# A hybrid GLA and MLA decoder block on one core: how far ahead the output stage loads its gates, and which PSUM banks its second pass uses

## The chip, the cores and the metric

The kernel runs on one core of a Trainium2 chip. The metric is device time in microseconds (us); the value shown for the kernel before is the median of three runs. An execution with the profiler on is shown beside it: all rows of the trace come from that one.

## The reference

One decoder block over 2048 frames and 16 learned meta tokens, width 1024, float32. Two token mixers run side by side on the same normalised input: a gated linear attention in chunks (its projected result is y_a) and a multi-head latent attention with softmax (its heads' result, gated, is o_b below). The part that the change touches is the end:

```
y_b    = (o_b * silu(m_z)) @ mla_proj
merged = sigmoid(gate_gla) * y_a + sigmoid(gate_mla) * y_b
h      = h + merged @ w_out
out    = rms_norm(h, final_norm_g)[:, 16:]
```

## The kernel before

All matrices are float32, and every product is made of three matmuls (`mm3`): each operand is split into a rounded part `hi` (a copy by ScalarE) and the rest `lo` (a subtraction, source minus hi), and hi·hi, hi·lo and lo·hi are summed in PSUM. The last stage is the class `Output`. It has two passes.

**First pass, `merge` (L1606).** It computes mergedᵀ, the 1024 channels in 8 blocks of 128 (`mo`) and the frames in 8 tiles of 256 (`t`): 64 products of 24 matmuls, 8 contraction blocks by 3. The first two products are already done inside the last unit of the attention (`first`). The weights of `mla_proj` stay on chip. For each product three arrays of 128 x 256 move between DRAM and the chip: `gm`, the raw gate of the latent branch, `ma`, the gated linear branch (both loaded), and the merged block, which is built in the `ma` tile and stored to `d_mg`. ScalarE makes the sigmoid of `gm` in three instructions (L134 to L136: exponential, logarithm, exponential), VectorE multiplies it with the product in PSUM (L1645) and adds it to `ma` (L1646). The pools set how far loads run ahead: `gm` has three tiles, `ma` four, and the products have four accumulators of one PSUM bank each, in two pools of two (`self.pa`). A tile is reused when its last reader is done; for `ma` that is the store. The code loads `gm` and `ma` at the head of the step that needs them; a scheduler at build time then sets the final order on each engine and on the queue of SyncE (SP below), which issues every DMA here. Each engine and the queue work in that order: an entry that waits holds up all behind it.

Within the same loop `load_ob` (L1585) loads and splits the attention result for the next frame tile in four pairs of blocks, through two raw tiles (`obr`); the `lo` half of every second block is made by GpSimd, except in tile 0. `blocks` (L1672) prepares the weights of the second pass in tiles 1 to 4: it loads two rows of blocks of `w_out` (`w_up`, `w_dn`) and makes four sums `f` of them (L1681 to L1684, the last two on GpSimd), which it splits. In tiles 5 to 7 `operands` begins to load and split merged blocks for the second pass.

**Second pass, `project` (L1730).** It computes merged @ w_out by a 2 x 2 scheme with seven block products in place of eight: 8 pairs of 128 frames (`p`), 7 products each of 12 matmuls with 512 columns, named by the weight block that they read: y11, t1, t2, t3, y21, t4, y22. Their accumulators `oacc` come from a pool of four PSUM banks (`self.pb`), opened in `merge` already. VectorE adds them up into rows (`o_row`), GpSimd adds the input rows `x_in`, and norm and store follow. The weight blocks y21, t4 and y22 are loaded and split at the head of the pass; four split operands (`xp`) are made ahead of the products.

Of the kernel before, what the change touches and what calls it, by code (L numbers as in the profile page):

```python
# [10 lines left out]
F32 = mybir.dt.float32  # L11
# [28 lines left out]
def f(ap):  # L40
    return ap.bitcast(F32)
# [1496 lines left out]
class Output:  # L1538
# [8 lines left out]
    def __init__(self, tc, x, mla_proj, w_out, final_g, out, S):  # L1547
        self.tc, self.nc, self.S = tc, tc.nc, S
        self.x, self.w, self.wo, self.fg, self.out = x, mla_proj, w_out, final_g, out
        self.right, self.left, self.psum = Pools(tc, "right"), Pools(tc), Pools(tc)  # L1550
        self.psum_r = Pools(tc)
        self.xp = self.right("d_xp", 4)
        self.raws = self.right("d_raw", 2)
        self.obr = self.right("d_obr", 2)
        self.weights, self.places, self.made = None, [], 0

# [28 lines left out]
    def load_ob(self, t, k, pool):  # L1585
# [4 lines left out]
        for i in range(2):  # L1590
            raw = self.obr.tile([P, W], F32, tag="ob", name="ob_raw")
            nc.sync.dma_start(raw, self.S.tr("ob", k + i)[:, t * W:(t + 1) * W])
            hi, lo = both[:, 0, i], both[:, 1, i]
            nc.scalar.activation(hi, raw, AF.Copy)
            (nc.vector if i == 0 or t == 0 else nc.gpsimd).tensor_sub(lo, raw, f(hi))
            got.append((hi, lo))
        return got

    def main(self):
# [3 lines left out]
        self.psum.close()  # L1603
        self.psum_r.close()

    def merge(self):  # L1606
# [6 lines left out]
        pools = [self.xp, self.left("d_ob2", 4)]  # L1613
        io, mp = self.left("d_io", 3), self.left("d_mg", 4)
        self.pa.append(self.psum("d_pa2", 2, space=PSUM))
        self.pb = self.psum("d_pb", 4, space=PSUM)
        tmp = Pools(self.tc)
        self.wraw, self.sums = tmp("d_wr", 1), tmp("d_ws", 1)
        stores = []
        for t in range(NTL):  # L1620
            cols = slice(t * W, (t + 1) * W)
            ob, self.obs = self.obs, []
# [6 lines left out]
            for mo in range(KC):  # L1629
                gm = io.tile([P, W], F32, tag="gm", name="gm")  # L1630
                nc.sync.dma_start(gm, S.tr("gm", mo)[:, cols])
                sigmoid(nc, gm, gm)
                ma = mp.tile([P, W], F32, tag="ma", name="ma")
                nc.sync.dma_start(ma, S.tr("ma", mo)[:, cols])
                if t == 0:
# [3 lines left out]
                else:  # L1639
                    acc = self.pa[(mo + 1) % 2].tile([P, W], F32, tag="a", name="acc")  # L1640
                    for kc in range(KC):
                        self.product(mo, acc, ob, kc)
                while len(stores) > 1:
                    nc.sync.dma_start(*stores.pop(0))
# [27 lines left out]
    def blocks(self, kc):  # L1672
# [9 lines left out]
        nc.vector.tensor_sub(t2, y22, t1)  # L1682
        nc.gpsimd.tensor_sub(t3, t2, y11)
        nc.gpsimd.tensor_sub(t4, y21, t2)  # L1684
        self.halves("y11", kc, y11, nc.vector)
# [44 lines left out]
    def project(self):  # L1730
# [7 lines left out]
        def rows(p):  # L1738
# [6 lines left out]
            return got  # L1745

        t4 = []
        for kc in range(KH):
# [3 lines left out]
            t4.append(raw)  # L1752
        xs = {0: rows(0)}
        y22 = []
        for kc in range(KH):
            self.halves("t4", kc, t4[kc], nc.vector)
            y22.append(self.w_piece(KH + kc, 1))
        for kc in range(KH):
            self.halves("y22", kc, y22[kc], nc.vector)
        fg = cst.tile([P, D], F32, name="fg")  # L1760
        nc.sync.dma_start(fg, self.fg.partition_broadcast(P))

        later, stores = [], []

        def product(right):
            acc = self.pb.tile([P, 512], F32, tag="b", name="oacc")
            while len(self.ready) < 4:
# [145 lines left out]
```

## Time and profile before

| | |
|---|---|
| Median of 3 runs | 2603.93 us (2601.11 to 2605.45) |
| Profiled execution, its own time | 2599.82 us |
| Span of its trace | 2598.1 us |
| TensorE matmul busy in the span | 2509.2 us (97%) |
| VectorE, ScalarE, GpSimd busy | 1670.7, 1363.1, 383.6 us |
| First pass from its third product on | 2217.6 to 2421.0 us |
| Second pass, matmuls | 2421.0 to 2589.0 us |

Times inside the trace count from the start of the span. A row of the waits says which engine and line stood idle, after the arrow what ended the wait, and then total, times and the longest. A matmul's end is modelled: in a dense run the next one begins before the one before it has ended.

### The profile page before, as it was taken

What the parts mean: (1) busy time and instruction counts of PE and PEld (TensorE: products, weight loads), DVE (VectorE), ACT (ScalarE), POOL (GpSimd) and SP (SyncE); (2) the same over time, 40 slices, a digit from 0 to 9 for tenths busy, and PEclk for the clock granted to TensorE, in tenths of its full rate; (3) what the DMA queues carried; (4) which work ended last, traced back from release to release, by engine and by line L of the source; (5) the groups of instructions that cost most, each with busy time, mean ns of one, the idle gap of its engine ahead of it and who ended that gap; (6) DMA issues with size and microseconds to landing.
All of it is one profiled execution on the core that took longest, in us unless ns stands there. A gap on an engine that the chain in (4) does not pass through costs nothing. (4 is left out here: it accounts for less than half of the span.)

```text
span 2598.1 us, 42674 instructions
## 1 busy us (share of the span) xinstructions
PE 2509.2 (97%) x14777; PEld 2218.5 (85%) x14777; DVE 1670.7 (64%) x3957; ACT 1363.1 (52%) x3210; POOL 383.6 (15%) x362
## 2 busy tenths in 40 slices
PE   7999999999999999999999999999999999988898
PEld 7998887878898888888877789999999999888776
DVE  7435878886624577786442487777776666553677
ACT  5323555774523375575354576655555555554433
POOL 2102332221301100000100010000000000221243
PEclk9999999999999999999999999999999999999999
DMA  5556776777357867777774331211111101675543
GB/s 147 169 155 230 259 243 207 245 242 237 109 177 226 242 220 252 233 245 223 230 221 142 108 113 62 70 44 39 41 37 34 37 26 38 208 224 167 188 153 115
DMA packets 320999, 413.04 MB, mean 159 GB/s; under 512 B 41968, under 2 KB 235808, under 8 KB 320784
## 3 DMA queue, kind: packets, MB, share of 16 engines
q1 hardware_dynamic: 320784, 410.33, 50.0%
q8 instruction: 116, 1.90, 0.3%
q14 instruction: 99, 0.81, 0.1%
HBM read 251.52 MB, written 158.68 MB: 158 GB/s over the span
## 5 line engine op out<-in xcount | busy, mean ns | idle before, releaser
L45 PE MATMUL acc<-t_hi,xp 128*128 128x512 f32 x640 | 254.6, 398 | 0.8 <-DMA xp<-d_xp 0.8
L47 PE MATMUL acc<-t_hi,xp 128*128 128x512 f32 x640 | 250.4, 391 | 0.0
L46 PE MATMUL acc<-t_lo,xp 128*128 128x512 f32 x640 | 249.8, 390 | 0.0
L46 PE MATMUL acc<-w_lo,y_hi 128*128 128x296 f32 (+1 forms) x640 | 194.6, 304 | 4.6 <-DVE w_lo L189 4.3
L47 PE MATMUL acc<-w_hi,y_lo 128*128 128x296 f32 (+1 forms) x640 | 193.8, 304 | 4.4 <-DVE y_lo L189 4.4
L45 PE MATMUL acc<-w_hi,y_hi 128*128 128x296 f32 (+1 forms) x640 | 194.6, 305 | 2.6 <-ACT y_hi L188 2.1
L45 PE MATMUL acc<-y_hi,xp 128*128 128x512 f32 x480 | 191.9, 400 | 0.0
L47 PE MATMUL acc<-y_hi,xp 128*128 128x512 f32 x480 | 188.0, 392 | 0.0
L1353 ACT ACTIVATE row<-row,nm,sr 128x144 f32<-128x144 f32 (+15 forms) x128 | 167.3, 1307 | 38.8 <-DVE nm L1352 35.5
L46 PE MATMUL acc<-y_lo,xp 128*128 128x512 f32 x480 | 187.5, 391 | 0.0
L1389 DVE TENSOR_TENSOR p_lo<-p_tp,p_hi 128x512 fp32r<-128x512 f32 x224 | 150.1, 686 | 48.6 <-ACT p_hi L1388 46.1
L1388 ACT ACTIVATE p_hi<-p_tp 128x512 fp32r<-128x512 f32 x224 | 129.2, 594 | 94.9 <-PE p_tp L1386 94.1
L1340 DVE TENSOR_SCALAR_CACHE_REDUCE row<-s 128x388 f32<-128x388 f32 (+13 forms) x224 | 130.8, 584 | 59.0 <-PE s L1338 56.8
L1386 PE MATMUL p_tp<-ident,row 128*128 128x128 f32 x1088 | 168.2, 273 | 0.0
L47 PEld LDWEIGHTS acc<-t_hi,xp 128*128 128x128 f32 x640 | 120.1, 188 | 25.8
L45 PEld LDWEIGHTS acc<-t_hi,xp 128*128 128x128 f32 x640 | 120.4, 188 | 24.6 <-issue 1.1
L1334 PE MATMUL s<-kt_hi,q_hi 128*128 128x420 f32 (+16 forms) x352 | 139.1, 395 | 1.9 <-DVE mx L1343 1.9
L1386 PEld LDWEIGHTS p_tp<-ident,row 128*128 128x128 f32 x1088 | 128.7, 140 | 14.2 <-ACT row L1353 4.5
L46 PEld LDWEIGHTS acc<-t_lo,xp 128*128 128x128 f32 x640 | 120.4, 188 | 22.3
L45 PE MATMUL o_acc<-p_hi,kn_hi 128*128 128x256 f32 x448 | 127.8, 285 | 1.0 <-ACT p_hi L1388 0.9
L46 PEld LDWEIGHTS acc<-w_lo,y_hi 128*128 128x128 f32 x640 | 122.4, 191 | 6.3 <-DVE w_lo L189 5.9
L46 PE MATMUL o_acc<-p_lo,kn_hi 128*128 128x256 f32 x448 | 126.7, 283 | 0.3
(416 smaller groups left out, 7446.9 us busy)
## 6 DMA issues: line engine op xcount, KB each, us to landing
d_xp<-xp SPq DMA_DIRECT2D x80, 512.0 KB
xp<-d_xp SPq DMA_DIRECT2D x80, 512.0 KB
w_raw<-in_w_in SPq DMA_DIRECT2D x60, 512.0 KB
xt<-in_x SPq DMA_DIRECT2D x16, 512.0 KB
d_z<-c SPq DMA_DIRECT2D x32, 256.0 KB
z<-d_z SPq DMA_DIRECT2D x64, 128.0 KB
v_hi<-d_vh SPq DMA_DIRECT2D x64, 128.0 KB
v_lo<-d_vl SPq DMA_DIRECT2D x64, 128.0 KB
```

The costliest lines, as they stand in the source:

```text
L45: nc.tensor.matmul(out, a_hi, b_hi, start=start, stop=False)
L46: nc.tensor.matmul(out, a_hi, b_lo, start=False, stop=False)
L47: nc.tensor.matmul(out, a_lo, b_hi, start=False, stop=stop)
L1334: nc.tensor.matmul(sv, q_hi[:, js], kt_hi[:, a:b], start=True, stop=False)
L1340: nc.vector.tensor_scalar(row[:, a:b], sv, 1.0, None, op0=ALU.mult, op1=ALU.max, accum_out=mx[:, i:i + 1])
L1353: nc.scalar.activation(row[:, :w], row[:, :w], AF.Exp, bias=nm, scale=sr[:, 4 * t + j:4 * t + j + 1], accum_out=rl[:, j:j + 1])
L1386: nc.tensor.transpose(tp[:, i, r * P:(r + 1) * P], rws[r][:, M + k * P:M + (k + 1) * P], ident)
L1388: nc.scalar.activation(fl(p_hi), fl(tp), AF.Copy)
L1389: nc.vector.tensor_sub(fl(p_lo), fl(tp), f(fl(p_hi)))
```

## The change

It has five parts.

- **Loads ahead.** A function `load` issues `gm` and `ma` for a product. At step n all loads up to product n + 3 are issued, `gm` has five tiles and `ma` six. The sigmoid of product n + 1 stands behind the matmuls of product n in the code.
- **VectorE for GpSimd.** The `lo` halves of `load_ob` and the sums t3 and t4 of `blocks` are all made by VectorE.
- **Raw tiles.** Within `merge`, `load_ob` has a pool of four raw tiles (`d_obr2`) in place of two.
- **Banks.** The pools of the first pass are closed at the head of `project`, and `oacc` then gets all eight banks; in place of the four of `self.pb`.
- **Splits of t4 and y22.** They stand in the code as steps between the first products (`later`) and no longer ahead of all of them, and the load of `final_norm_g` (`fg`) stands ahead of them.

```
-            (nc.vector if i == 0 or t == 0 else nc.gpsimd).tensor_sub(lo, raw, f(hi))
+            nc.vector.tensor_sub(lo, raw, f(hi))
...
-        io, mp = self.left("d_io", 3), self.left("d_mg", 4)
+        io, mp = self.left("d_io", 5), self.left("d_mg", 6)
+        self.obrs.append(self.left("d_obr2", 4))
         self.pa.append(self.psum("d_pa2", 2, space=PSUM))
-        self.pb = self.psum("d_pb", 4, space=PSUM)
...
+        def load(t, mo):
+            cols = slice(t * W, (t + 1) * W)
+            gm = io.tile([P, W], F32, tag="gm", name="gm")
+            nc.sync.dma_start(gm, S.tr("gm", mo)[:, cols])
+            ma = mp.tile([P, W], F32, tag="ma", name="ma")
+            nc.sync.dma_start(ma, S.tr("ma", mo)[:, cols])
+            return gm, ma
...
-                gm = io.tile([P, W], F32, tag="gm", name="gm")
-                nc.sync.dma_start(gm, S.tr("gm", mo)[:, cols])
-                sigmoid(nc, gm, gm)
-                ma = mp.tile([P, W], F32, tag="ma", name="ma")
-                nc.sync.dma_start(ma, S.tr("ma", mo)[:, cols])
+                while len(got) < min(n + 4, KC * NTL):
+                    got.append(load(*divmod(len(got), KC)))
+                if n == 0:
+                    sigmoid(nc, got[0][0], got[0][0])
+                gm, ma = got[n]
...
+                if n + 1 < len(got):
+                    sigmoid(nc, got[n + 1][0], got[n + 1][0])
+                n += 1
...
-        nc.gpsimd.tensor_sub(t3, t2, y11)
-        nc.gpsimd.tensor_sub(t4, y21, t2)
+        nc.vector.tensor_sub(t3, t2, y11)
+        nc.vector.tensor_sub(t4, y21, t2)
...
+        self.psum.close()
+        self.psum_r.close()
+        pb = self.psum("o_ps", 8, space=PSUM)
...
-        later, stores = [], []
+        later = [[lambda b=b, k=k: b(k), lambda b=b, k=k + 1: b(k)]
+                 for b, k in ((t4_block, 0), (t4_block, 2), (y22_block, 0), (y22_block, 2))]
+        stores = []
...
-            acc = self.pb.tile([P, 512], F32, tag="b", name="oacc")
+            acc = pb.tile([P, 512], F32, tag="b", name="oacc")
```

SP's queue in frame tiles 6 and 7, before; the number behind `d_gm` and `d_ma` begins with the channel block, and ma_28779, ma_28823 and ma_28858 are the blocks 4, 5 and 6 of tile 6:

```order
L1644 DMA d_mg3_314<-ma_28779 128x256
L1631 DMA gm_28888<-d_gm7_113 128x256
L1634 DMA ma_28928<-d_ma0_122 128x256
L1644 DMA d_mg3_314<-ma_28823 128x256
L1631 DMA gm_28923<-d_gm0_106 128x256
L1634 DMA ma_28963<-d_ma1_123 128x256
L1644 DMA d_mg3_314<-ma_28858 128x256
L1631 DMA gm_28958<-d_gm1_107 128x256
```

The same place after; ma_28668 and ma_28703 are again the blocks 4 and 5 of tile 6:

```order
L1624 DMA gm_28868<-d_gm1_107 128x256
L1626 DMA ma_28870<-d_ma1_123 128x256
L1655 DMA d_mg3_314<-ma_28668 128x256
L1624 DMA gm_28903<-d_gm2_108 128x256
L1626 DMA ma_28905<-d_ma2_124 128x256
L1655 DMA d_mg3_314<-ma_28703 128x256
L1624 DMA gm_28938<-d_gm3_109 128x256
L1626 DMA ma_28940<-d_ma3_125 128x256
```

Behind the store of block 4 stood the gate of block 7, three products later; now the gate of block 2 of the next tile stands there, six later. The load of `ma` still follows the store that frees its tile with one load between them.

TensorE where the second pass begins, before:

```order
L46 MATMUL acc_29197<-ob_28809,wv_hi3_15497 128x256
L47 MATMUL acc_29197<-ob_28809,wv_lo3_15501 128x256
L45 MATMUL oacc_29315<-oy11_hi_26611,xp_29032 128x512 [waits Activation_49]
L46 MATMUL oacc_29315<-oy11_lo_26612,xp_29032 128x512
L47 MATMUL oacc_29315<-oy11_hi_26611,xp_29032 128x512
```

And after:

```order
L46 MATMUL acc_29197<-ob_28824,wv_hi3_15497 128x256
L47 MATMUL acc_29197<-ob_28824,wv_lo3_15501 128x256
L45 MATMUL oacc_29297<-oy11_hi_26611,xp_29047 128x512 [waits DVE_49]
L46 MATMUL oacc_29297<-oy11_lo_26612,xp_29047 128x512
L47 MATMUL oacc_29297<-oy11_hi_26611,xp_29047 128x512
```

The order is the same, but the first matmul now waits for VectorE: in the built program for the multiplication of the first pass's last product, whose bank pool was closed.

VectorE in the first pair of frames of the second pass, from the evacuation of product t2 on, before (oy22_lo is the `lo` half of weight block y22, sa and sb are sums of merged blocks for the next pair):

```order
L1824 TENSOR_TENSOR u2_29345<-oacc_29346,o_row_29312 128x512
L1705 TENSOR_TENSOR xp_29369<-sa_29367,xp_29369 128x512
L1825 TENSOR_TENSOR o_row_29312<-oacc_29329,u2_29345 128x512
L1670 TENSOR_TENSOR oy22_lo_29265<-wo_raw_29288,oy22_hi_29264 128x512
L1670 TENSOR_TENSOR oy22_lo_29265<-wo_raw_29292,oy22_hi_29264 128x512
L1829 TENSOR_TENSOR o_row_29313<-oacc_29366,u2_29345 128x512
L1670 TENSOR_TENSOR oy22_lo_29265<-wo_raw_29296,oy22_hi_29264 128x512
L1670 TENSOR_TENSOR oy22_lo_29265<-wo_raw_29300,oy22_hi_29264 128x512
L1830 TENSOR_TENSOR o_row_29313<-oacc_29329,o_row_29313 128x512
L1705 TENSOR_TENSOR xp_29397<-m_raw_29393,xp_29397 128x512
L1836 TENSOR_TENSOR o_row_29312<-oacc_29392,o_row_29312 128x512
L1838 TENSOR_TENSOR o_row_29313<-oacc_29413,o_row_29313 128x512
```

After:

```order
L1842 TENSOR_TENSOR u2_29343<-oacc_29344,o_row_29294 128x512
L1716 TENSOR_TENSOR xp_29371<-sa_29369,xp_29371 128x512
L1843 TENSOR_TENSOR o_row_29294<-oacc_29319,u2_29343 128x512
L1681 TENSOR_TENSOR oy22_lo_29266<-wo_raw_29313,oy22_hi_29265 128x512
L1681 TENSOR_TENSOR oy22_lo_29266<-wo_raw_29317,oy22_hi_29265 128x512
L1847 TENSOR_TENSOR o_row_29295<-oacc_29368,u2_29343 128x512
L1681 TENSOR_TENSOR oy22_lo_29266<-wo_raw_29337,oy22_hi_29265 128x512
L1848 TENSOR_TENSOR o_row_29295<-oacc_29319,o_row_29295 128x512
L1681 TENSOR_TENSOR oy22_lo_29266<-wo_raw_29341,oy22_hi_29265 128x512
L1716 TENSOR_TENSOR xp_29403<-m_raw_29399,xp_29403 128x512
L1854 TENSOR_TENSOR o_row_29294<-oacc_29398,o_row_29294 128x512
L1721 TENSOR_TENSOR sa_29420<-m_raw_29399,m_raw_29401 128x512
```

Of the four halves of y22 only the last has moved, behind one more evacuation, and the sum sa has come ahead of the evacuation of t4 (L1856, the next row).

## Rows read from the trace of the kernel before

**Rows 1.** Section 1 of the page: busy us, share of span, instructions.

```profile
PE 2509.2 (97%) x14777; PEld 2218.5 (85%) x14777; DVE 1670.7 (64%) x3957; ACT 1363.1 (52%) x3210; POOL 383.6 (15%) x362
```

**Rows 2.** Stretches: length, each engine's busy us, granted clock, DMA share, GB/s.

```profile
2357.00:2361.00 4.00, 3.46 (x16) 3.46 (x17) 2.33 (x6) 1.97 (x5) 0.72 (x1) 0.57 0.38 115
2449.00:2453.00 4.00, 3.49 (x9) 2.57 (x10) 2.28 (x4) 2.02 (x4) 1.60 (x1) 0.58 0.27 107
2217.00:2421.00 204.00, 183.18 (x1488) 178.74 (x1489) 93.45 (x183) 105.78 (x266) 39.22 (x41) 0.98 0.65 199
2421.00:2454.00 33.00, 27.28 (x111) 21.02 (x110) 22.38 (x36) 17.26 (x36) 8.46 (x6) 0.95 0.67 214
2454.00:2589.00 135.00, 131.15 (x565) 105.19 (x563) 101.42 (x176) 50.88 (x121) 56.88 (x41) 1.00 0.42 139
```

**Rows 3.** Waits of TensorE in the first pass, 2217 to 2421.

```profile
PE acc L45 <- DVE gm L1645: 17.7, 15, 3.6
PE acc L45 <- ACT ob L1594: 1.5, 1, 1.5
PE acc L45 <- DVE rb L1443: 0.9, 1, 0.9
PE acc L46 <- POOL ob L1595: 0.7, 2, 0.4
```

**Rows 4.** Waits of VectorE, ScalarE and SP's queue in the first pass.

```profile
DVE gm L1645 <- ACT gm L136: 33.5, 21, 4.1
...
ACT gm L134 <- DMA gm<-d_gm: 65.2, 41, 5.1
...
SPq L1634 <- DMA d_mg<-ma: 32.3, 28, 4.0
```

**Rows 5.** Timeline, TensorE: start, length, instruction; in brackets idle time before it.

```profile
2226.48 0.39 PE L45 MATMUL acc<-ob,kt_lo 128*128 128x256 f32 x1 [1.45 <-DVE gm L1645]
...
2231.64 0.28 PE L46 MATMUL acc<-ob,kn_hi 128*128 128x256 f32 x1
...
2232.46 0.28 PE L47 MATMUL acc<-ob,kn_lo 128*128 128x256 f32 x1
...
2357.54 0.58 PE L45 MATMUL acc<-ob,kst 128*128 128x256 f32 x1 [3.60 <-DVE gm L1645]
```

**Rows 6.** Timeline of SP's queue late in the first pass.

```profile
2398.59 0.38 SPq L1644 DMA_DIRECT2D d_mg<-ma  x1
...
2400.95 0.32 SPq L1634 DMA_DIRECT2D ma<-d_ma  x1
2401.36 0.38 SPq L1644 DMA_DIRECT2D d_mg<-ma  x1
```

**Rows 7.** Instructions of L1645, L1646 and L1595: duration ns min/median/max.

```profile
L1645 DVE TENSOR_TENSOR gm<-acc,gm x61: 409/417/426, 2226.0 to 2419.1; 128x256 f32<-128x256 f32 x61
L1646 DVE TENSOR_TENSOR ma<-ma,gm x61: 411/425/1278, 2226.5 to 2419.6; 128x256 f32<-128x256 f32 x61
...
L1595 DVE TENSOR_TENSOR ob<-ob_raw,ob x28: 412/426/1486, 2222.8 to 2390.7; 128x256 fp32r<-128x256 f32 x28
```

**Rows 8.** Waits of TensorE from 2421 to 2454 (three), from 2454 to 2589 (one).

```profile
PE oacc L45 <- DVE u L1824: 2.3, 1, 2.3
PE oacc L45 <- ACT xp L1704: 1.9, 1, 1.9
PE oacc L45 <- DVE o_row L1829: 1.6, 1, 1.6
...
PE oacc L45 <- DVE o_row L1829: 3.8, 5, 1.1
```

**Rows 9.** Timeline around the change of passes, and the last split of y22.

```profile
2421.01 0.40 PE L45 MATMUL oacc<-oy_hi,xp 128*128 128x512 f32 x1
...
2427.39 0.42 DVE L1645 TENSOR_TENSOR gm<-acc,gm 128x256 f32<-128x256 f32 x1 [2.12 <-ACT gm L136]
2427.84 0.43 DVE L1646 TENSOR_TENSOR ma<-ma,gm 128x256 f32<-128x256 f32 x1
...
2443.12 0.69 DVE L1670 TENSOR_TENSOR oy_lo<-wo_raw,oy_hi 128x512 fp32r<-128x512 f32 x1 [0.89 <-ACT oy_hi L1669]
```

More of the change, by code (lines that the diff above doesn't have):

```diff
@@ L1554, in __init__ @@
         self.obr = self.right("d_obr", 2)
+        self.obrs = [self.obr]
         self.weights, self.places, self.made = None, [], 0
@@ L1590, in load_ob @@
         for i in range(2):
-            raw = self.obr.tile([P, W], F32, tag="ob", name="ob_raw")
+            raw = self.obrs[-1].tile([P, W], F32, tag="ob", name="ob_raw")
             nc.sync.dma_start(raw, self.S.tr("ob", k + i)[:, t * W:(t + 1) * W])
@@ L1603, in main @@
         self.psum.close()
-        self.psum_r.close()
     def merge(self):
@@ L1613, in merge @@
         pools = [self.xp, self.left("d_ob2", 4)]
-        io, mp = self.left("d_io", 3), self.left("d_mg", 4)
+        io, mp = self.left("d_io", 5), self.left("d_mg", 6)
+        self.obrs.append(self.left("d_obr2", 4))
         self.pa.append(self.psum("d_pa2", 2, space=PSUM))
-        self.pb = self.psum("d_pb", 4, space=PSUM)
         tmp = Pools(self.tc)
         self.wraw, self.sums = tmp("d_wr", 1), tmp("d_ws", 1)
-        stores = []
+        stores, got, n = [], [], 0
+        def load(t, mo):
[5 more added lines that the diff above has]
+            return gm, ma
         for t in range(NTL):
-            cols = slice(t * W, (t + 1) * W)
             ob, self.obs = self.obs, []
@@ L1753, in project, with t4_block, y22_block @@
         xs = {0: rows(0)}
+        fg = cst.tile([P, D], F32, name="fg")
+        nc.sync.dma_start(fg, self.fg.partition_broadcast(P))
         y22 = []
-        for kc in range(KH):
+        def t4_block(kc):
             self.halves("t4", kc, t4[kc], nc.vector)
             y22.append(self.w_piece(KH + kc, 1))
-        for kc in range(KH):
+        def y22_block(kc):
             self.halves("y22", kc, y22[kc], nc.vector)
-        fg = cst.tile([P, D], F32, name="fg")
-        nc.sync.dma_start(fg, self.fg.partition_broadcast(P))
-        later, stores = [], []
+        later = [[lambda b=b, k=k: b(k), lambda b=b, k=k + 1: b(k)]
+                 for b, k in ((t4_block, 0), (t4_block, 2), (y22_block, 0), (y22_block, 2))]
+        stores = []
         def product(right):
-            acc = self.pb.tile([P, 512], F32, tag="b", name="oacc")
+            acc = pb.tile([P, 512], F32, tag="b", name="oacc")
             while len(self.ready) < 4:
```

## The prediction

> **What bounds the kernel now.** The page comes first: TensorE has matmuls in flight for 97% of the span [rows 1], so only its idle time and its slow clock can be won, some 3%. The table of stretches comes second, because the change touches nothing before 2217 us. The first pass of the output stage lasts 203.4 us (2217.6 to 2421.0) for 1488 matmuls [rows 2]. In a dense run seven matmuls start within 0.82 us, 0.117 us each [rows 5], so 1488 of them need 174.1 us: about 29 us of this pass are lost. In the second pass the first 33 us hold 27.3 us of matmul, the remaining 135 us hold 131.2 [rows 2]: about 10 more. Third, the waits say who is late. In the first pass TensorE waits 15 times, 17.7 us in all, for the multiplication L1645 [rows 3]: the bank that it wants still holds a product that VectorE has not read. VectorE was itself waiting for the sigmoid, and the sigmoid for the load of gm, 65.2 us in 41 waits [rows 4]. So it is the late gate that holds the banks. The reader is to see this chain, gm, sigmoid, multiplication, bank, and that its last link alone counts. Right after an idle stretch the granted clock reads 0.57 over 4 us [rows 2], that is, mostly the lower level of 1.2 GHz in place of 2.4: 0.43 x 4 = 1.7 us lost each time. The one at 2357 us follows on a wait of 3.60 us [rows 5], the longest of the pass [rows 3]; the one at 2449 us follows on the three waits at the start of the second pass [rows 8].
>
> **The change, part by part.** A wait's row counts from the modelled end of the matmul before it, 0.28 us after its start, where the next could have started after 0.12 [rows 5]; so each wait costs 0.16 us more than its row says. In the second pass a matmul's row is 0.40 us [rows 9] and the pace 131.15/565 = 0.23 [rows 2], so 0.17.
>
> *Loads ahead.* Before, a gm tile comes free when the product three back is added, so a load, its sigmoid, multiplication and addition have 3 x 24 x 0.117 = 8.4 us to go round. With five tiles they have 14.0 us, which is 5.6 more, and the longest bank wait is 3.6 [rows 3]. The order bears it out: behind the store of block 4 of a tile stands the gate of six products later, where it was three. I take all bank waits as gone but the first: at 2226.48 us TensorE waits 1.45 us [rows 5] for the very first gate, whose place in the queue is unchanged. 17.7 - 1.45 + 14 x 0.16 = **18.5 us** won. Bounds: 0 if SP is no earlier for other reasons (rival B), 20.1 if the first goes too. With the idle 3.6 us the slow clock behind it goes: **1.7 us** (0 to 1.7).
>
> *Splits from GpSimd to VectorE, and four raw tiles.* TensorE waits 1.5 + 0.7 us for ob halves [rows 3], 2.7 with the restarts, nearly all where tile 1 begins. Four raw tiles let the loads start earlier, but in the new order the last four halves of tile 1 stand behind the multiplication of product 7, after which only 2.1 us pass until block 6 is needed. I take **1.5 us** won (0 to 2.7). VectorE takes on 28 halves of 0.43 us [rows 7] and 8 sums of twice that width, 18.9 us, on 93.5 of 204 [rows 2]: 112 of some 183, 61%, so I put it at nothing; its cover is the four banks, which let VectorE lag by three products, 8.4 us. The row of L1646, which reads two operands on chip, goes from 0.41 to 1.28 us, that of L1645, with one operand in PSUM, never over 0.43 [rows 7], and GpSimd was busy for 39 us beside them [rows 2].
>
> The Trainium skill's page "SBUF — State Buffer" (Who interferes with whom) says that a VectorE instruction with two SBUF inputs contends with a GpSimd one that reads SBUF, through a shared read interface, and one with a single such input does not. The two rows agree; by that rule VectorE's added load is partly paid back, which lowers the chance of rival B and leaves the sum as it is.
>
> *Banks.* In the second pass bank waits are those on L1824 and L1829: 2.3 and 1.6 us at the start, then five of 3.8 us in all [rows 8], at one product per pair. With eight banks a product waits for the one eight back, no longer four. The five: 3.8 + 5 x 0.17 = **4.6 us** won (0 to 4.6). The three at the start, with the wait for xp (1.9), are 5.8 + 0.5 = 6.3 us. They have two causes: few banks, and a VectorE that comes late. It ends the first pass at 2428.3 us, 7.3 us after TensorE [rows 9], because the last gates are late too; everything of the second pass queues behind that, and the last half of y22 is ready at 2443.8 us, 22.8 after the pass began [rows 9]. With the gates early, multiplication and addition end about 1.1 us after the last product, and y22 is ready at about 16.6; it is the seventh product, due at 6 x 12 x 0.23 = 16.6 us. That fits with no margin, so I leave 1 us standing: **5.3 us** won (0 to 6.3), and the slow clock of 2449 us with it, **1.7 us** (0 to 1.7).
>
> *The price of the banks.* The first matmul of the second pass now waits for the multiplication of the last product. No row of now shows this wait; the nearest is that for L1443, a multiplication that frees the bank between two products, 0.9 us [rows 3]. That one is 512 wide, this one 256, 0.42 us [rows 9]: about 0.65 + 0.16 = **0.8 us** lost (0 to 3.6, the longest bank wait). *Splits of t4 and y22 as steps:* the order of VectorE moves one half of y22 behind one evacuation and little else; nothing, between 0 and 0.7 us won.
>
> Sum: 18.5 + 1.7 + 1.5 + 4.6 + 5.3 + 1.7 - 0.8 = 32.5 us. From it I take 1.5 us, one bank wait with its restart, for a pause of SP that the lead does not cover: **31 us**. The profiled execution took 2599.8 us (span 2598.1) and would take 2569; the median of the runs is 4.1 us higher, so I forecast **2573 us**.
>
> **Rivals.**
>
> *B, SP's queue sets the pace.* The load of ma still waits until the store that frees its tile has come back, and still stands right behind it. Late in the pass store to store takes 2401.36 - 2398.59 = 2.77 us [rows 6], a product on TensorE 24 x 0.117 = 2.81. So a lead once lost hardly grows again, and every entry that does not fit beside a store under way costs its issue. For it: 28 such waits, 32.3 us [rows 4]. Against it: most other entries (ob loads, gates) stand between a store and its load and so cost nothing, and the lead of four products, 11 us, is there at the start. If half of the bank waits stay: 32.5 - 9.3 = 23 us, **2581 us**.
>
> *C, the second pass still begins late*, since the weight loads stand behind the same waits as before: 5.3 and 1.7 us missing, **2580 us** with the rest of the forecast.
>
> *D, slower.* The same place with a dearer store: more loads under way at once lengthen a store's return by x, the pass then takes 62 x (2.77 + x). It is slower than now from 203.4 + 10.8 us on, 10.8 being what the second pass gains; that is x = 0.68 us. At x = 1: 233.7 us, 19.5 us over the whole, **2623 us**. For it: a wait for a store of 4.0 us has occurred [rows 4]. Against it: the bytes are the same, the mean wait is 32.3/28 = 1.15 us at a DMA share of 0.65 [rows 2, 4].
>
> The Trainium skill's page "DMA: Bandwidth & Descriptors" (Latency and other measured facts) puts HBM latency at 0.2 us on average and 2 us at high load, and makes it the larger part of a transfer's fixed cost. By that rule x could be up to 1.8 us, 62 x 4.57 = 283 us for the pass and about 2673 us as an estimate from that page; the 2.77 us cycle [rows 6] does not bear out such a rise at the load of now, and no run here yet shows the higher one.
>
> *E, nothing comes of it:* the waits move to the ob halves or to VectorE in full, **2604 us**.
>
> **How the numbers follow.** Forecast 0.62, with its own range 2566 to 2577 (1.5 us of pause or none, bounds of the small terms). B 0.19, C 0.13, D 0.03, E 0.03. The range 2564 to 2587 holds forecast and C and most of B. A measurement of this kernel tells 0.2%, 5.2 us, from no change. Faster by more than that: forecast, B and C and a little less than all of them, 0.94; within it 0.03; slower 0.03.
>
> **What would show it.** Right: in the first pass TensorE's waits for the multiplication fall from 15 to one or two, at its start; ScalarE's waits for gm nearly vanish; the granted clock is full from 2222 us on to the end; the first pass lasts about 183 us, the matmuls of the second 157; at the change of passes stands one new wait under 1 us on the multiplication. B would show as SP waits for d_mg with TensorE's bank waits behind them late in the pass; C as waits for xp or for halves of t4 and y22 within 25 us of the change; D as stores that come back after 3 us and more. The forecast is wrong if the first pass is not shorter by at least 15 us.

## The result and the profile after

The changed kernel takes 2589.45 us (median of 4 runs, 2583.78 to 2591.12); the kernel before took 2603.31 beside it. The ratio is 0.9943, 95% interval 0.9926 to 0.996: 14 us faster. The forecast was 2573 with a range from 2564 to 2587, so the sign was right and less than half of the 31 us came.

The profiled execution took 2589.68 us (span 2587.9), where the forecast for it was 2569. Section 1 of its page and four stretches (columns as in [rows 2]):

```profile
PE 2511.8 (97%) x14777; PEld 2222.5 (86%) x14777; DVE 1672.2 (65%) x3993; ACT 1363.5 (53%) x3210; POOL 349.0 (13%) x326
```

```profile
2222.00:2415.00 193.00, 180.76 (x1488) 178.62 (x1488) 96.92 (x223) 109.89 (x273) 4.93 (x5) 0.97 0.69 214
2415.00:2578.00 163.00, 157.06 (x672) 125.32 (x672) 123.61 (x205) 63.56 (x147) 65.45 (x46) 1.00 0.48 155
2230.00:2237.00 7.00, 6.15 (x29) 6.15 (x30) 3.07 (x8) 6.17 (x18) 0.00 (x0) 0.51 0.77 244
2380.00:2384.00 4.00, 4.00 (x24) 4.00 (x23) 3.15 (x9) 1.73 (x5) 0.00 (x0) 0.57 0.70 159
```

The passes begin and end at these matmuls of the timeline:

```profile
2221.82 0.38 PE L45 MATMUL acc<-ob,kt_hi 128*128 128x256 f32 x1 [0.85 <-DVE rb L1443]
...
2415.24 0.50 PE L45 MATMUL oacc<-oy_hi,xp 128*128 128x512 f32 x1 [0.59 <-DVE gm L1656]
...
2577.86 0.40 PE L47 MATMUL oacc<-oy_hi,xp 128*128 128x512 f32 x1
```

So the first pass lasts 193.4 us (203.4 before, 183 forecast), the second 163.0 (168.0 and 157), and the first pass begins 4.2 us later than before. TensorE's waits in the first pass, to set beside [rows 3]:

```profile
PE acc L45 <- DVE gm L1656: 11.8, 8, 3.1
...
PE oacc L45 <- DVE gm L1656: 0.6, 1, 0.6
```

The wait for the multiplication (L1656 now) fell from 15 times to 8, from 17.7 to 11.8 us. With the prediction's own prices the pass adds up: 174.1 in a dense run, 11.8 + 8 x 0.16 = 13.1 for these waits, 0.8 for the one at the change of passes, and 0.49 x 7 + 0.43 x 4 = 5.1 for two stretches near the lower clock level, each behind a wait: 193.1 of the 193.4. Of the eight waits the first (3.1 us) is the one that the prediction left standing. The other seven begin between 2317 and 2377 us. The waits of the other engines in the pass, to set beside [rows 4]:

```profile
ACT gm L134 <- DMA gm<-d_gm: 49.3, 36, 3.5
DVE ob L1596 <- ACT ob L1595: 34.6, 23, 7.6
DVE gm L1656 <- ACT gm L136: 13.9, 7, 6.5
DVE sa L1721 <- DMA m_raw<-d_mg: 10.5, 1, 10.5
DVE f L1692 <- DMA w_up<-in_w_out: 9.0, 4, 5.3
```

```profile
SPq L1626 <- DMA d_mg<-ma: 45.7, 37, 3.3
```

Two things are to be seen. VectorE waits for a late gate only 13.9 us (33.5 before), but beside that for copies of ob and for loads that have nothing to do with gates. And SP's queue waits for stores 45.7 us in 37 of 64 steps, where it was 32.3 in 28. First VectorE and ScalarE around two of the waits, with the last matmul of the second one's product:

```profile
2308.24 0.42 ACT L136 ACTIVATE gm<-gm 128x256 f32<-128x256 f32 x1
...
2317.17 0.69 DVE L1692 TENSOR_TENSOR f<-w_up 128x512 f32<-128x512 f32 x1 [5.32 <-DMA w_up<-in_w_out]
...
2319.27 0.42 DVE L1656 TENSOR_TENSOR gm<-acc,gm 128x256 f32<-128x256 f32 x1
...
2334.55 0.42 ACT L136 ACTIVATE gm<-gm 128x256 f32<-128x256 f32 x1
...
2336.11 0.28 PE L47 MATMUL acc<-ob,kn_lo 128*128 128x256 f32 x1
...
2345.08 0.69 DVE L1721 TENSOR_TENSOR sa<-m_raw 128x512 f32<-128x512 f32 x1 [10.50 <-DMA m_raw<-d_mg]
...
2346.42 0.42 DVE L1656 TENSOR_TENSOR gm<-acc,gm 128x256 f32<-128x256 f32 x1
```

The gate multiplied at 2319.27 was ready at 2308.66, that of 2346.42 at 2334.97; their products were complete at 2309.6 and 2336.4. So both multiplications came some 10 us after both, behind an instruction on VectorE placed ahead of its data: a sum for a w_out block, and the first sum for the second pass. (At 2377 us it is halves of ob, twice: they waited 7.6 us for their copies on ScalarE, behind the sigmoid of a gate three products on, and the gate for SP; then 3.9 us for copies whose own load was late.) Four banks cover 8.4 us. The Trainium skill's page "Perfetto Trace Analysis" (Tensor Engine Instruction) says that ScalarE, VectorE and GpSimd take their instructions in strict order; the 10.50 us agree.

It is the same at all seven: the gate was done at most 2.1 us after the product, and the multiplication came 9.7 to 11.0 us after both. In the kernel before, at the fourteen waits behind the first, the gate came 4.7 to 9.3 us after its product, and the multiplication another 0.7 to 6.8 us after the gate. The wait of 3.60 us [rows 5] there (last matmul of the product, its gate, VectorE):

```profile
2343.95 0.28 PE L47 MATMUL acc<-ob,wq_lo 128*128 128x256 f32 x1
...
2352.84 0.42 ACT L136 ACTIVATE gm<-gm 128x256 f32<-128x256 f32 x1
...
2356.73 0.43 DVE L1595 TENSOR_TENSOR ob<-ob_raw,ob 128x256 fp32r<-128x256 f32 x1 [5.49 <-ACT ob L1594]
2357.07 0.42 DVE L1645 TENSOR_TENSOR gm<-acc,gm 128x256 f32<-128x256 f32 x1
```

So the late gates are gone, and what now holds the banks is what stands ahead of the multiplications on VectorE.

Now SP's queue, two steps:

```profile
2366.90 0.42 SPq L1655 DMA_DIRECT2D d_mg<-ma  x1
2367.41 0.38 SPq L1624 DMA_DIRECT2D gm<-d_gm  x1
2369.25 0.32 SPq L1626 DMA_DIRECT2D ma<-d_ma  x1
2369.62 0.42 SPq L1655 DMA_DIRECT2D d_mg<-ma  x1
2370.14 0.38 SPq L1624 DMA_DIRECT2D gm<-d_gm  x1
2373.38 0.32 SPq L1626 DMA_DIRECT2D ma<-d_ma  x1
2373.74 0.43 SPq L1655 DMA_DIRECT2D d_mg<-ma  x1
```

The load of `ma` still waits for the store issued just ahead of its gate. Three products ahead, the one at work and two by which a store lags make six, so the tile asked for is always the one just sent off. Store to store takes 2.72 us, then 4.12, a product 2.81: rival B's loop. Other loads stand behind it: that of the merged rows for the sum at 2345.08 was issued at 2339.84, behind a load of `ma` that came 3.15 us after its gate (2339.00 and 2335.85). In the second pass the waits on o_row [rows 8] are gone and another stands once in each pair (columns of the first row as above; then the timeline of one case):

```profile
PE oacc L47 <- DVE xp L1716: 5.5, 7, 1.3
```

```profile
2484.84 2.74 DVE L1822 SCALAR_TENSOR_TENSOR y<-o_row,rs,fg 128x512 f32<-128x512 f32 x4
2487.50 1.29 DVE L1716 TENSOR_TENSOR xp<-m_raw,xp 128x512 fp32r<-128x512 f32 x2
2488.24 0.50 PE L47 MATMUL oacc<-oy_hi,xp 128*128 128x512 f32 x1 [0.73 <-DVE xp L1716]
```

### The profile page after: what moved, and what is told of

The parts are those of the page before. It is cut to its first block, busy times and chain, and to the rows that moved or that the text cites. A ratio compares the mean times of both kernels' runs of the same rounds, so it can differ in the third digit from the quotient of the medians.

```text
span 2587.9 us, 42585 instructions
## 1 busy us (share of the span) xinstructions
PE 2511.8 (97%) x14777; PEld 2222.5 (86%) x14777; DVE 1672.2 (65%) x3993; ACT 1363.5 (53%) x3210; POOL 349.0 (13%) x326
## 4 chain that ended last, share of the span: by engine, by line
PE 64%; DMA 11%; DVE 11%; ACT 7%; issue 4%; POOL 2%; SPq 1%; POOLq 0%; DVEq 0%; ACTq 0%
PE acc L45 11%; PE acc L47 11%; PE acc L46 11%; PE p_tp L1386 4%; PE o_acc L46 3%; PE o_acc L45 3%; PE o_acc L47 2%; PE s L1334 2%; PE s L1338 2%; PE s L1337 2%; PE s L1336 2%; PE s L1335 2%; DMA d_mg<-ma 2%; DVE xp L189 1%; DMA w_raw<-in_w_in 1%
## 5 line engine op out<-in xcount | busy, mean ns | idle before, releaser
L47 PE MATMUL acc<-t_hi,xp 128*128 128x512 f32 x640 | 251.0, 392 | 0.0
L47 PE MATMUL acc<-w_hi,y_lo 128*128 128x296 f32 (+1 forms) x640 | 193.5, 303 | 4.3 <-DVE y_lo L189 4.3
L47 PE MATMUL acc<-y_hi,xp 128*128 128x512 f32 x480 | 188.1, 392 | 0.0
L47 PEld LDWEIGHTS acc<-t_hi,xp 128*128 128x128 f32 x640 | 120.6, 188 | 26.0
L47 PEld LDWEIGHTS acc<-w_hi,y_lo 128*128 128x128 f32 x640 | 121.5, 190 | 5.6 <-DVE y_lo L189 5.5
```

Source lines behind the costliest of these rows:

```text
L47: nc.tensor.matmul(out, a_lo, b_hi, start=False, stop=stop)
```

## The experiments

Sixteen runs, four to a chip, each beside the kernel before. Pass lengths are from the one profiled execution of each; in a_first and a_gates half a product of the first pass, 1.4 us, stands ahead of the point from which it is measured.

| Kernel | median us | ratio to before, 95% | pass 1 | pass 2 |
|---|---|---|---|---|
| before | 2602.6 to 2604.7 | | 203.4 | 168.0 |
| a_again: changed kernel again | 2588.0 | 0.9942 (0.9926 to 0.9957) | 194.8 | 162.5 |
| b_second: before, new second pass | 2605.5 | 1.0011 (1.0002 to 1.0019) | 211.0 | 162.6 |
| b_ahead: before, loads ahead | 2597.3 | 0.9974 (0.9964 to 0.9985) | 202.3 | 161.9 |
| a_4banks | 2587.9 | 0.9943 (0.9924 to 0.9961) | 196.2 | 161.9 |
| a_raw2 | 2592.7 | 0.9965 (0.9953 to 0.9977) | 198.6 | 161.9 |
| a_gp | 2592.3 | 0.9959 (0.9947 to 0.9971) | 197.4 | 162.5 |
| a_first | 2587.5 | 0.9934 (0.9917 to 0.995) | 193.0 | 162.4 |
| a_fin3 | 2586.1 | 0.9938 (0.9925 to 0.995) | 190.6 | 160.5 |
| a_ma8 | 2582.2 | 0.9922 (0.9909 to 0.9934) | 189.8 | 162.0 |
| a_gps | 2598.8 | 0.9979 (0.9969 to 0.999) | 203.1 | 160.4 |
| a_ma8_gps | 2597.7 | 0.9974 (0.9962 to 0.9986) | 200.5 | 162.6 |
| a_held | 2598.2 | 0.9977 (0.9966 to 0.9989) | 199.2 | 165.4 |
| a_ma8_held | 2579.8 | 0.9916 (0.9898 to 0.9934) | 184.1 | 163.0 |
| the same again | 2577.1 | 0.9905 (0.9892 to 0.9918) | 184.1 | 162.6 |
| a_best | 2582.5 | 0.9921 (0.9904 to 0.9938) | 186.7 | 162.5 |
| a_gates | 2583.0 | 0.9921 (0.9906 to 0.9935) | 188.5 | 162.9 |

### Does the later start belong to the change?

> The changed kernel once more, nothing edited. In its profiled execution the third product of the first pass began at 2221.8 us, 4.2 us later than in the kernel before, although nothing ahead of it was changed; there were 20.4 us of half granted clock ahead of that point against 6.8. Theory V: this differs from execution to execution. Then a new execution has another set of such stretches ahead of 2217 us, and its third product begins where these put it: about 2214.2 us plus half of their total length. Rival K: it belongs to the kernel (its tiles lie elsewhere). Then the same stretches come again and the third product begins within 0.5 us of 2221.8. By both, the waits of the first pass cluster again between 2317 and 2377 us and the median stays at 2588 to 2591.

The stretches are others, as V had it: from 650 to 656 us the granted clock was 0.50 in the first execution of the changed kernel and 1.00 in the new one. The new execution had 13.7 us of half clock ahead of the first pass in place of 20.5, yet this began at 2222.2 us, not at 2221.0 as V's rule expected, and within the 0.5 us that K allowed. But a_fin3, which differs in the second pass alone, began at 2219.7 with the same 13.7. Over all 18 profiled executions the first pass began between 2217.6 and 2224.7 us, roughly the later the more half clock lay ahead, but with the same 13.7 us anywhere from 2217.7 to 2222.2. So the start is no mark of the change; what settles it beside the clock stays open. Against both theories the waits did not keep their places: seven again follow the first, but between 2299 and 2402 us.

### The parts alone

> The kernel before with the second pass of the changed one (eight banks, splits of t4 and y22 as steps, fg earlier) and the first pass left as it was. By the terms of the prediction that do not rest on early gates (five bank waits 4.6, price of the new wait 0.8) it gains 3.8 us: 2599.5; with the start of the pass as well (5.3 and 1.7) 10.8 us: 2592.5. Rival X: the bank waits turn into waits for the split operands, about as long, as the profile after suggests (5.5 us in 7 waits in place of 3.8 in 5): then it gains nothing or loses, 2601 to 2605.

The second pass grafted onto the kernel before, with its eight banks and steps. It is slower, 1.0011. Its matmuls take 162.6 us in place of 168.0, but all of that is paid ahead of them:

```profile
PE oacc L45 <- DVE gm L1643: 7.1, 1, 7.1
```

This is the new wait of the change of passes, priced at 0.8 us. With late gates VectorE ends the first pass 7 us after TensorE [rows 9]; four banks of their own let the second pass begin meanwhile, eight shared ones do not. Rival X is right in the time (2605.5, just above its range), for another reason: its waits for xp are there too (3.6 us in 5 waits, where there were 3.8 in 5 for banks), but the 7.1 us decide.

> The kernel before with the loads three products ahead alone (five gm tiles, six ma tiles, the sigmoid one product ahead); GpSimd keeps its halves and sums, two raw tiles, four banks. By the prediction's terms 18.5 and 1.7 us: 2583. If it carries what the whole change gave, 14 to 15 us: 2589. Rival R: the halves from GpSimd to VectorE and the four raw tiles are needed for it, since an ob half on GpSimd holds its raw tile and with it the queue that the gates stand in: 2594 to 2600.

```
+        io, mp = self.left("d_io", 5), self.left("d_mg", 6)
...
+                while len(got) < min(n + 4, KC * NTL):
+                    got.append(load(*divmod(len(got), KC)))
...
+                if n + 1 < len(got):
+                    sigmoid(nc, got[n + 1][0], got[n + 1][0])
```

7.4 us. The first pass hardly moves (202.3 us), and the gain lies where the second begins: 161.9 us with four banks. Rival R fits in the time, but it was not the gates that were held. At the twelve waits for the multiplication behind the first one the gate was done at most 3.2 us after its product, and the multiplication came 8.4 to 12.5 us after both. One of them:

```profile
2349.49 0.28 PE L47 MATMUL acc<-ob,wq_lo 128*128 128x256 f32 x1
...
2351.63 0.42 ACT L136 ACTIVATE gm<-gm 128x256 f32<-128x256 f32 x1
...
2358.15 0.42 ACT L134 ACTIVATE gm<-gm 128x256 f32<-128x256 f32 x1 [2.02 <-DMA gm<-d_gm]
...
2360.71 0.43 DVE L1595 TENSOR_TENSOR ob<-ob_raw,ob 128x256 fp32r<-128x256 f32 x1 [6.63 <-ACT ob L1594]
...
2361.38 0.42 DVE L1656 TENSOR_TENSOR gm<-acc,gm 128x256 f32<-128x256 f32 x1
...
2361.86 0.39 PE L45 MATMUL acc<-ob,kn_hi 128*128 128x256 f32 x1 [2.72 <-DVE gm L1656]
```

VectorE waited for a copy of ob, and ScalarE made that copy behind the sigmoid of a later product, which waited for its load. Early gates alone do not free the banks.

> The changed kernel with the second pass put back on four banks of its own, opened in the first pass; all else as changed. By the prediction's terms five bank waits come back (4.6) and the new wait at the change of passes goes (0.8): 3.8 us more, 2592. Rival X: bank waits and waits for split operands (5.5 us in 7 waits now) are the same lateness of VectorE seen at two places, so the second pass is as long with four banks as with eight: 2587 to 2590. In both cases the start of the second pass shows what early gates alone do: its three waits (5.8 us before) are gone by the first, still there if they were for want of banks.

```
+        self.pb = self.psum("d_pb", 4, space=PSUM)
...
-        pb = self.psum("o_ps", 8, space=PSUM)
+        pb = self.pb
```

Nothing: 0.9943 as with eight, and a second pass of 161.9 us. The five bank waits are back at their old length, and the waits for xp on L47 gone but for one of 0.7 us:

```profile
PE oacc L45 <- DVE o_row L1847: 3.8, 5, 0.9
```

Rival X holds: bank waits and operand waits are one lateness of VectorE seen at two places, and the waits at the start of the pass went through early gates, not through banks.

> The changed kernel with two raw tiles for the loads of ob in the first pass, as in the kernel before; all else as changed. The loads ahead alone gave 7.4 us, the whole change 14.7, eight banks nothing; so 7 to 9 us must come from the halves on VectorE, the four raw tiles, or both, where the prediction had put 1.5. Theory T: it is the raw tiles. A load of ob waits in SP's queue until the half two back is made, and the gates wait behind it: 2595 (2593 to 2598). Theory V: it is the place where the halves are made (a half on GpSimd takes 1.3 us and stands behind a ScalarE copy), then two tiles do nearly as well: 2588 to 2590.

```
-        self.obrs.append(self.left("d_obr2", 4))
+        self.obrs.append(self.left("d_obr2", 2))
```

> The changed kernel with every second half of ob and the sums t3 and t4 made by GpSimd again, as in the kernel before; four raw tiles kept. By theory T (raw tiles) the time stays at 2587 to 2590. By theory V (VectorE in place of GpSimd) the gain of 7 to 9 us goes: 2595. By the prediction, which put both together at 1.5 us, both runs stay within 2588 to 2590.

```
-            nc.vector.tensor_sub(lo, raw, f(hi))
+            (nc.vector if i == 0 or t == 0 else nc.gpsimd).tensor_sub(lo, raw, f(hi))
```

(t3 and t4 on GpSimd as well.) Both undo about as much: against 0.9942 the ratios rise by 0.0023 and 0.0017, 6.0 and 4.4 us. Each interval overlaps that of a_again by a little; b_ahead and a_4banks, 8 us apart, say more, and differ by little else than these two edits. So neither theory alone: raw tiles and the engine of the halves both seem to carry the first pass, and the prediction's 1.5 us for the two was several times too small. (A half on GpSimd took 0.74 us in the median, not 1.3.)

### What holds the multiplications after 2310 us

> The changed kernel with eight ma tiles in place of six; the loads are issued no earlier than before (three products ahead). Theory S: the load of ma waits for the store that was issued directly ahead of its gate (45.7 us in 37 waits of SP's queue), this round trip of 2.4 us and some issue paces the queue, and the lead is used up by tile 4. With two more tiles the load waits for a store two products older, which is long back: SP's waits there fall from 45.7 to under 10 us, TensorE's seven waits for the multiplication after 2310 us (8.7 us, 9.8 with the restarts, and 1.5 of slow clock behind the last) go, the first pass lasts about 182 us, the median 2578 (2574 to 2582). Rival N: the late loads come from the number of DMA instructions and from VectorE, not from the stores. Then the wait moves to another entry of the queue and the time stays at 2586 to 2591.

```
-        io, mp = self.left("d_io", 5), self.left("d_mg", 6)
+        io, mp = self.left("d_io", 5), self.left("d_mg", 8)
```

```profile
SPq L1626 <- DMA d_mg<-ma: 21.8, 18, 3.2
```

5.8 us faster than the changed kernel run beside it (the intervals overlap by a little), between the two theories. SP's waits halve, but waits for the multiplication stay, from 2316, 2340 and 2367 us on among others. In the built order the loads of `ma` now run further ahead, late in the pass up to two products ahead of their gates, so some of them follow the store of their own tile closely again. S is one cause of two; that it is one is shown by the pair of kernels with the order kept, further down.

> The changed kernel with everything that waits for a load of weights or of merged rows taken from VectorE's queue in the first pass: the four sums and the lo halves of the w_out blocks (32 instructions) and the first pair's two sums sa and sb are made by GpSimd. Theory H: the waits of TensorE after 2310 us come from VectorE's queue, which works in order: a sum that waits 5.3 us for w_up (2317) and one that waits 10.5 us for merged rows (2345) stand ahead of multiplications whose gates were ready up to 11 us before. Without them the waits at 2317 to 2330 (3.6 us) and at 2344 to 2357 (3.1 us) go, 7.7 us with the restarts; the one at 2377, behind halves of ob, stays. Median 2580 (2577 to 2583). Rival S: the gates are late through the loop of store and load; then VectorE waits for the gate where it now waits for w_up and for the merged rows, and the time stays at 2586 to 2590.

```
-        nc.vector.tensor_sub(t1, y12, y11)
+        nc.gpsimd.tensor_sub(t1, y12, y11)
...
-        self.halves("y11", kc, y11, nc.vector)
+        self.halves("y11", kc, y11, nc.gpsimd)
```

Slower by some 10 us (0.9979 against 0.9942), which neither theory expected. The waits of VectorE are gone, as H had it, and came back through ScalarE, whose copies of the sums now wait for GpSimd, with a sigmoid and the copies of ob behind them:

```profile
ACT ot_hi L1680 <- POOL f L1693: 9.2, 4, 3.0
```

```profile
2290.03 0.63 ACT L1680 ACTIVATE ot_hi<-f 128x512 fp32r<-128x512 f32 x1 [2.38 <-POOL f L1693]
...
2292.35 0.51 DVE L1596 TENSOR_TENSOR ob<-ob_raw,ob 128x256 fp32r<-128x256 f32 x1 [9.74 <-ACT ob L1595]
2292.78 0.41 DVE L1656 TENSOR_TENSOR gm<-acc,gm 128x256 f32<-128x256 f32 x1
```

Everything waits in a line: w_up, GpSimd, ScalarE, VectorE, and with it TensorE for 3.83 us at 2293. Moving the late instruction to another engine moved the line, not the lateness.

> As before (sums and halves of the w_out blocks and the first pair's sums on GpSimd), and eight ma tiles. Eight tiles alone gave 2582.2. Theory H with S beside it: both add up, as they act at different places: about 2574.5. Rival: they are the same microseconds (a gate that comes earlier waits for VectorE, a VectorE that is free waits for the gate): 2580 to 2582.

2597.7: eight tiles do not help where the lines are these.

> The changed kernel; the four sums and the splits of the w_out blocks and the first pair's operands keep, on VectorE and ScalarE, their place in the order of the code (behind the multiplication of the product beside which they are written); nothing is moved to another engine. With these on GpSimd the time had risen by 11 us, with ScalarE then waiting for GpSimd (9.2 us). Theory H: what holds the multiplications after 2310 us is instructions that stand on VectorE and ScalarE ahead of their data: a sum for w_up (5.3 us) and one for merged rows (10.5 us). Placed later, they find their data there: these two waits of VectorE fall under 1 us each, TensorE's waits at 2317 to 2330 and 2344 to 2357 go (7.7 us with restarts): 2580 (2577 to 2583). Rival S: the gates are late through the loop of store and load, and the multiplications then wait for them at the same places: 2586 to 2590.

```
+        nc, KH, pin = self.nc, KC // 2, self.tc.keep_in_program_order
...
-        nc.vector.tensor_sub(t1, y12, y11)
+        pin(nc.vector.tensor_sub(t1, y12, y11))
```

(The same for all four sums, the splits of the blocks, and the first pair's operands.) VectorE's two waits are gone from its list, and yet the kernel is 9 us slower. SP's loop has grown a little (48.8 us in 45 waits for stores), and the last wait is the dearest (TensorE's waits from 2416 us on; VectorE's timeline ahead of them):

```profile
PE oacc L45 <- DVE gm L1656: 5.2, 1, 5.2
```

```profile
2415.06 0.69 DVE L1716 TENSOR_TENSOR xp<-sa,xp 128x512 fp32r<-128x512 f32 x1 [8.18 <-ACT xp L1715]
2415.67 0.42 DVE L1656 TENSOR_TENSOR gm<-acc,gm 128x256 f32<-128x256 f32 x1
```

The two lines that held VectorE before are gone and a third holds it, a split of the first operands, ahead of the last four multiplications. So H names what happens, but keeping the order is no remedy by itself.

> The same order kept, with eight ma tiles (these alone gave 2582.2). Theory H with S beside it: both act, 2575 (2572 to 2578). Rival: they are the same microseconds, 2580 to 2583.

> The kernel with eight ma tiles and the order kept once more, beside the three above on the same chip. It settles whether 2579.8 and the first pass of 184.1 us hold, or whether that execution was a lucky one: 2578 to 2582 and 183 to 187 us if they hold, 2582 to 2588 and 188 us or more if not.

Both changes together: 2579.8 and, run again, 2577.1. The first pass lasts 184.1 us in both executions. From the second one:

```profile
2218.93 0.58 PE L45 MATMUL acc<-ob,kt_hi 128*128 128x256 f32 x1 [0.85 <-DVE rb L1443]
...
2402.98 0.47 PE L45 MATMUL oacc<-oy_hi,xp 128*128 128x512 f32 x1 [0.61 <-DVE gm L1656]
```

```profile
PE acc L45 <- DVE gm L1656: 5.1, 6, 1.6
```

```profile
SPq L1626 <- DMA d_mg<-ma: 15.1, 18, 1.7
```

Here is the first pass that the prediction had forecast (183 us). With six tiles the order kept costs 9 us, with eight it gains 1.6 to 4.4 (0.9916 and 0.9905 against 0.9922: the intervals overlap; passes of 184.1, 184.1 and, in a_best below, 186.7 us stand against one of 189.8). That eight tiles are needed for it is shown: 0.9977 with six, 0.9916 and 0.9905 with eight.

### Smaller waits, and putting all together

> The changed kernel; the last part of the normalisation of a pair of frames (four multiplications of 0.69 us on VectorE) is cut into two steps, so that a split of an operand stands between the two halves. Theory Y: in the second pass TensorE waits once in each pair for that split (5.5 us in 7 waits, 6.7 with the restarts), because the four multiplications, 2.74 us, stand ahead of it on VectorE. With 1.37 us less ahead of it (the longest wait is 1.3) these waits fall under 1 us and the time by 5 to 6.5 us: 2583.5. Rival F: VectorE is full in this stretch and only the place of the wait changes (to an evacuation or to the second split), time 2587 to 2591.

```
+                if i:
+                    yield
```

```profile
PE oacc L47 <- DVE xp L1716: 2.0, 6, 0.4
```

The second pass loses 2 us (160.5), the time 1.9, with an interval that overlaps. Y is right about the cause, but 3.5 us less of waits shorten the pass by 2.0 only, and 1.3 of these are eaten at the end: there GpSimd's last sum, not TensorE, releases the last norm, and the tail is 11.0 us long in place of 9.7.

> The changed kernel; only the gate of product 0 has a tile of its own and is loaded during the attention, so its sigmoid is done before the first pass begins. Theory Q: the wait for the first multiplication (3.1 us in the profiled execution of the changed kernel, 3.5 with eight ma tiles) is a matter of that load's place in the queue, behind the store of the last attention block; it goes, with the half clock behind it (3.4 to 6.8 us at half speed): 4 to 6 us less, 2583. Rival: the gates of products 1 and 2 are as late and two products further on TensorE waits for these: 0 to 1.5 us less.

The rival was right: the wait moved to the bank of product 1, two products on (2.05 us at 2230.13), and the time stayed (2587.5).

> All that the experiments point to: the changed kernel with eight ma tiles, the order kept for blocks and first operands, and the normalisation of a pair in three steps (alone 1.9 us, half of its gain in the second pass lost again in a tail of 11.0 us in place of 9.7). If the parts add up: 2573 to 2575. If not: 2578 to 2582.

2582.5: the parts do not add up; three steps of the norm bring nothing on top. The order in the first pass is that of the kernel run beside it, on every engine and in the queue, so its 186.7 us against 184.1 differ by execution alone.

> The order kept for blocks and first operands (which with eight ma tiles gave 2579.8 and a first pass of 184.1 us), the gates of products 0 and 1 loaded during the attention into tiles of their own, seven ma tiles and one raw tile less in the attention, for want of room. If the wait for the first gate (3.3 us, with 1.5 us of half clock behind it) goes and seven tiles do as well as eight: 2575 to 2577. If the first gates move work in the attention, or seven tiles hold the queue as six do: 2582 to 2598.

```
+        self.gates = [self.g0.tile([P, self.W], F32, tag="gm0", name="gm") for _ in range(2)]
...
-        self.obr = self.right("d_obr", 2)
+        self.obr = self.right("d_obr", 1)
```

2583.0, 5.9 us more than the kernel with eight tiles beside it. SP waits for stores 21.9 us in place of 15.1, and 2.5 us of waits for ob are new; which of seven tiles and the one raw tile costs more was not tried apart. The fastest kernel stays the one with eight ma tiles and the order kept, 2577 to 2580 us, by the ratios 7 to 10 us faster than the changed one.

## Why the prediction was wrong

Against 2569 the profiled execution took 20.7 us more: 10.4 in the first pass, 6.0 in the second, 4.2 by the later start, 0.5 in the tail (0.4 too many, as the forecast lengths are rounded). The forecast of 2573 had allowed 4.1 us for the profiled execution being a quick one, about as much as the start took; the rest is the miss.

*Loads ahead, 18.5 and 1.7 us:* the step that failed. It took "all bank waits as gone but the first", because it took the late gate for the only thing that holds the banks. The gates did come early, in b_ahead as in the changed kernel, and 11.8 of the 17.7 us stayed: at the seven late waits the multiplication came 9.7 to 11.0 us after its gate and its product, behind other instructions on VectorE. The kernel before showed the sign of it in a row that [rows 4] leave out, VectorE's longest waits in the pass:

```profile
DVE ob L1595 <- ACT ob L1594: 44.1, 20, 5.5
```

The step also counted the gm tiles and not the ma tiles. `ma` goes round through a store, and with six tiles the load waits for the store just issued, and all other loads of SP's queue with it; a_ma8 puts this at 5.8 us. b_ahead measured 7.4 us in all and next to nothing in the first pass. Rival B described this loop, with the price of half the bank waits staying (11.8 of 17.7 stayed); it was given 0.19 because "the lead of four products, 11 us, is there at the start". It is there, and it is used up by tile 4: after the first no such wait until 2317 us, then seven (until 2299 us in a_again). But that the waits move "to the ob halves or to VectorE" is rival E, given 0.03; each of the seven shows its mechanism, and B's loop feeds it. That ScalarE's waits for gm would nearly vanish was the wrong sign to look for: they stay at 49.3 us, and at 48.2 in the kernel with the pass of 184.1 us, mostly ScalarE running ahead of its need. B's 2581 was still too low, as it left the bank terms standing.

*VectorE at nothing, covered by four banks:* wrong as well, and the other half of the same miss. The cover is 8.4 us, the instructions on VectorE and ScalarE that stood ahead of their data held the multiplications for 9.7 to 11.0. The prediction added up busy time (61%) where the order of the queue counted, although [rows 4] show VectorE waiting 33.5 us in its queue for another engine's result. With both mended, by eight ma tiles and the order kept, the pass lasts 184.1 us; what the order adds to the eight tiles (1.6 to 4.4 us) is not clear of the noise.

*Splits and raw tiles, 1.5 us:* mis-sized. From b_ahead to a_4banks, which differ by these edits, the order of the splits of t4 and y22 and the load of `fg`, 0.9974 falls to 0.9943, 8 us; undone by themselves they cost 4.4 and 6.0, each uncertain by about as much. The term priced only TensorE's own waits for ob, not what the raw tiles hold up in SP's queue.

*Five bank waits, 4.6 us:* nothing, shown by a_4banks; rival E's mechanism in small. *Start of the second pass, 5.3 and 1.7:* right in size, 6.1 us in b_ahead, and right in cause (early gates). *The new wait, 0.8:* right, 0.6 and restart, as long as the gates are early; 7.1 in b_second, where they are not. The upper bound of 3.6 was too low: the nearest row for it was VectorE's end in [rows 9], 7.3 us after TensorE's.

*Rival D:* not borne out. At a DMA share of 0.69 a wait for a store took 45.7/37 = 1.24 us on average, 3.3 at most, against 1.15 and 4.0. The Trainium skill's page "DMA: Bandwidth & Descriptors" (Latency and other measured facts) puts HBM latency at up to 2 us at high load; these waits show no such rise.

*VectorE beside GpSimd:* VectorE's sum with two inputs on chip took up to 1.51 us beside GpSimd in a_gps and at most 0.43 otherwise, but the relief was not what decided. The Trainium skill's page "SBUF — State Buffer" (Who interferes with whom) says that such an instruction contends with a GpSimd one that reads SBUF; the two durations agree.

## What to carry to other kernels

Before crediting a lead, go round each ring of tiles separately, stores included: the products ahead, the one at work and those by which the store lags (3 + 1 + 2 here) are a count of tiles at which each load falls on the tile just sent off; with two more the queue's waits for stores halved. Early inputs are not enough: engines that work in order pass on each other's lateness, so ask of every instruction ahead of the one that matters what *its* data wait for; busy shares say nothing of it, and moving it to another engine, as tried here, moved the line. A remedy can cost time alone and not beside another (the order kept: 9 us lost with six tiles, none with eight), so test the pair before dropping either.

## What was not expected of the hardware

Stretches of 3.4 or 6.8 us at the lower clock level come at other places in each execution, also of the same kernel (6.8 to 23.9 us in all ahead of the first pass, over 18 profiled executions), and the same point of the program is reached up to 7 us earlier or later. A gain of that size in one profiled execution, or a later start, is no evidence. Lengths of single passes held somewhat better: with the same order on every engine the first pass took 193.4, 194.8 and 190.6 us (the changed kernel twice, a_fin3), and 184.1, 184.1 and 186.7 us (eight tiles with the order kept, twice, and a_best).
